# Additions out of PSUM in a seven-product down projection, marked urgent for VectorE's order

## The chip, the cores and the metric

The kernel runs on one core of one Trainium2 chip. The metric is the device time of one execution in microseconds (us), taken as the median of several runs. The core's engines each work through a queue of their own: TensorE (PE, with its weight loads as PEld), VectorE (DVE), ScalarE (ACT), GpSimd (POOL), and SyncE (SP), which issues the transfers. A scheduler in the programming layer fixes each queue's order when the program is built; at run time semaphores alone make one engine wait for another.

## What is computed

A two-layer encoder trunk over 512 + 256 tokens (two request groups, T = 768 columns here) of width 1024. Layer 0 mixes with a Fourier transform, layer 1 with a gated DeltaNet; after each mixer comes a SwiGLU channel mixer, whose second product the change touches:

```python
def swiglu(h, w_gu, w_down):
    gu = h @ w_gu
    return (jax.nn.silu(gu[..., :FFN_DIM]) * gu[..., FFN_DIM:]) @ w_down
...
        x = x + g2 * swiglu(h, ffn_w_gu[layer], ffn_w_down[layer])
```

FFN_DIM is 2816, 22 blocks of 128. `g2` is a gate per output column and request group.

## The kernel before

The residual x lies transposed in eight tiles of 128 x 768 (`xs`, called `x` in layer 0; in layer 1 the same eight are borrowed tiles, `pad`, `qT`, `vT`, `we`, `wa`). Every matrix product is made in three passes of reduced-precision parts: a weight block is split into `wh` (rounded by ScalarE) and `wl` (the rest, a subtraction on DVE); so is the activation.

The hidden blocks are worked in groups of four (`PARTS`). `gate_up` makes the gate and up blocks of one hidden block, "a unit": seven products instead of eight of a 2 x 2 block scheme, each 12 matmuls of 384 columns. `down4` then takes a group of four hidden blocks into four of the eight output blocks, again with seven products of a 2 x 2 scheme, named 1 to 7 and run in the order 1, 2, 6, 7, 5, 4, 3. Each product has two halves (`i`, two output blocks of 128) of 6 matmuls. A group needs two calls, `m0` = 0 and 4; the first runs after the first unit of the next group, the second after that group's second unit (`pending`). With five groups of four in layer 0 and four in layer 1 there are 18 calls.

The products add up in six PSUM banks: two each of `pw` (product 2), `py` (7, then 4 on top) and `px` (1, then 6, 5 and 3 on top). A product that goes on top may start in a bank only when the sum so far has been read out of it. `into` is the reader in question, on DVE: it multiplies the bank by the gate and adds it to x. `low(row)` is one addition of 384 columns (tokens 0 to 383), `high(row)` one of 128 and one of 256 (the two request groups in tokens 384 to 767). `shared` reads on ScalarE and adds on GpSimd.

DVE's queue holds, around a call: the weight splits of `down4` itself (line 498) and of the next unit (`split_w`, line 152), combinations of weight blocks (`comb`, lines 492 and 379, some of them on GpSimd), the activations' work of `gate_up` and `take`, and the additions of `into` (line 532 before, 533 after). Splits, combinations and ScalarE's reads are already built inside `tc.high_priority()`, which makes the scheduler take them first among those ready on an engine; the additions of `into` are not. Up to five weight blocks are held (`WP`), so a split may stand well ahead of its product.

Of the kernel before, what the change touches and what calls it, by code (L numbers as in the profile page):

```python
# [15 lines left out]
ALU = mybir.AluOpType  # L16
# [93 lines left out]
def encoder_kernel(  # L110
# [5 lines left out]
    V, A_, G = nc.vector, nc.scalar, nc.gpsimd  # L116
# [58 lines left out]
    def bank(pool, g=None):  # L175
        if pool.name == "ppr1":
            return pool.tile([P, SEGS[g][1]], F32, name=f"pr{g}", bufs=2 - g)
        return pool.tile([P, 512], F32, name="pr")

    def passes(ps, w, ah, al, first=True, **kw):  # L180

        kc = len(ah)
        for k in range(kc):
            for n, (a, b) in enumerate(((w[0], ah), (w[0], al), (w[1], ah))):
                last = mm(ps, a[k], b[k], start=(first and k == 0 and n == 0), stop=(k == kc - 1 and n == 2), **kw)
            yield last
# [18 lines left out]
    modT = const.tile([P, 14, KC, 2], F32, name="modT")  # L205
# [271 lines left out]
    def down4(l, c0, m0, rights, xs, psp, wk):  # L477

        w2d = ffn_w_down[l]

        def fetch2(m):
            stg = weights["stg"].tile([P, KC, P], F32, name="stg")
            nc.sync.dma_start(stg.rearrange("p (k m) n -> p k (m n)", m=2),
                              w2d[c0 * P : (c0 + 4) * P, m * P : (m + 2) * P].rearrange("(k p) n -> p k n", p=P))
            return stg.rearrange("p (k m) n -> p k m n", m=2)

        def four(t):
            return t.rearrange("p (k m) n -> p k m n", m=2)

        def comb(eng, out, a, b, op):  # L490
            with tc.high_priority():
                eng.tensor_tensor(out, a, b, op)

        def parts(src):
            wh, wl = (four(weights[name].tile([P, HK, P], F32R, name=name)) for name in ("wh", "wl"))
            with tc.high_priority():
                A_.copy(wh, src)  # L497
                V.tensor_tensor(wl, src, wh.bitcast(F32), ALU.subtract)  # L498
            return wh, wl

        def left():
            s_a, s_b = fetch2(m0), fetch2(m0 + 2)
            a11, a12, a21, a22 = s_a[:, 0::2], s_a[:, 1::2], s_b[:, 0::2], s_b[:, 1::2]
            yield parts(a11)
            yield parts(a12)
            s1 = four(wk.tile([P, HK, P], F32, name="s1", bufs=WS))
            comb(G, s1, a21, a22, ALU.add)
            comb(G, a21, a11, a21, ALU.subtract)
            comb(V, a11, s1, a11, ALU.subtract)
            yield parts(a11)  # L510
            yield parts(a21)
            yield parts(s1)
            yield parts(a22)
            comb(V, a12, a12, a11, ALU.subtract)
            yield parts(a12)

        lefts = left()
        pw, py, px = ([bank(psp) for _ in range(2)] for _ in range(3))
        gate = GATE[2 * l + 1]

        def run(n, ps, first, then):
            wh, wl = next(lefts)
            for i in range(2):
                for _ in passes(ps[i][:, :HT], ([wh[:, k, i] for k in range(2)], [wl[:, k, i] for k in range(2)]),
                                [r[n][0] for r in rights], [r[n][1] for r in rights], first, skip_group_check=True):
                    pass
                then(i, ps[i])

        def into(m, ps, a, b, g):
            x = xs[m][:, a:b]  # L530
            o = HT if a >= HT else 0
            V.scalar_tensor_tensor(x, ps[:, a - o : b - o], modT[:, gate, m, g : g + 1], x, ALU.mult, ALU.add)  # L532

        def low(row):
            return lambda i, ps: into(m0 + 2 * row + i, ps, 0, HT, 0)

        def high(row):
            def fn(i, ps):
                into(m0 + 2 * row + i, ps, HT, S0, 0)
                into(m0 + 2 * row + i, ps, S0, T, 1)  # L540
            return fn

        def shared(row):
            def fn(i, ps):
                m = m0 + 2 * row + i
                t = wk.tile([P, HT], F32, name="m7", bufs=M7)
                with tc.high_priority():
                    A_.activation(t, ps[:, :HT], AF.Copy, scale=modT[:, gate, m, 0:1])
                G.tensor_tensor(xs[m][:, LO], xs[m][:, LO], t, ALU.add)
            return fn  # L550

        run(1, px, True, shared(0))
        run(2, pw, True, low(0))
        run(6, px, False, shared(1))
        run(7, py, True, high(1))
        run(5, px, False, high(1))
        run(4, py, False, low(1))
        run(3, px, False, high(0))
# [65 lines left out]
    with ExitStack() as l0:  # L624
# [8 lines left out]
        with ExitStack() as fs:  # L633
# [41 lines left out]
            for c in range(KC):  # L675
                pcs.append(fp.tile([P, NC + NS], F32, name="xt", bufs=8))
                ps = pbig.tile([P, 1024], F32, name="big")
                oc, os_ = 0, 512
                for g, s in ((0, S0), (1, S1)):
                    for par in (0, 1):  # L680
# [3 lines left out]
                        for kt in range(nkt):  # L684
                            o, n = COLS[f"seq{g}_{kt}_{par}"]
# [13 lines left out]
            for c in range(KC):  # L699
# [7 lines left out]
                o, n = COLS["cosd"]  # L707
                mm(pf[:, 0:NC], ftab[:, o : o + n], y[:, :NC])
                o, n = COLS["sind"]
# [605 lines left out]
```

## Time and profile before

| | |
|---|---|
| median of 3 runs | 1961.96 us (1960.85 to 1962.16) |
| the profiled execution | 1961.55 us, span 1959.8 us |
| busy | PE 94%, PEld 84%, DVE 75%, ACT 50%, POOL 29% |
| mean granted TensorE clock | 0.984 |
| calls of `down4` in layer 0 | first at 257.9 us, last ends at 729.4 us |
| calls of `down4` in layer 1 | first at 1545.9 us, last ends at 1868.5 us |

A row of the timeline gives start and duration in us, engine, line, operation, output<-inputs by the program's names with buffer numbers left out, shapes, count, and in brackets the idle time before it and what ended that. `g` are the activations in `down4`'s matmuls, `pr` is any PSUM bank. Rows of "who waited" give us in total and times. A row of windows gives the stretch, its length, and for PE, PEld, DVE, ACT and POOL the busy time with the number of instructions, then the granted clock, the DMA engines' share and GB/s. Matmuls overlap: each is written some 0.34 us long, but the next starts 0.17 us after it.

### The profile page before, as it was taken

Reading aid. Unit: us, or ns where it says so; the run is one execution under the profiler, and the core shown is the slowest. Engines: PE = TensorE matmul, PEld = TensorE weight load, DVE = VectorE, ACT = ScalarE, POOL = GpSimd, SP = SyncE. Lnnn points to the kernel's source line nnn. Section 1 sums busy time; section 2 is a strip of 40 time slices with the busy share of each in tenths; the row PEclk is TensorE's granted clock in tenths of the full one; section 3 lists DMA queues with packets and bytes.
Section 4 is the critical chain, followed back from the end, with each engine's and each line's share of the span. In section 5 each row is a group of like instructions: output and inputs, shape, how many; then the busy total and the mean of one; then the engine's idle time right before and its main releaser. Section 6 shows DMA issues by size and latency. Waiting matters only on the chain.

```text
span 1959.8 us, 30027 instructions
## 1 busy us (share of the span) xinstructions
PE 1842.1 (94%) x11281; PEld 1636.7 (84%) x11281; DVE 1468.8 (75%) x2399; ACT 977.8 (50%) x1858; POOL 563.7 (29%) x454
## 2 busy tenths in 40 slices
PE   8899999999999998999999999899789999999998
PEld 5585998888897986888888888778589999999998
DVE  4638877777786767896887787773778888888875
ACT  3526544444443535756656557543554444444543
POOL 1314333233242310122213212320432333433431
PEclk9999999999999998999999999999899999999999
DMA  7654334433425434421222222241213222222211
GB/s 268 215 183 140 86 97 130 127 116 114 139 87 153 126 113 141 119 51 56 69 60 65 66 62 57 61 142 38 53 41 89 68 77 72 65 65 68 77 50 65
DMA packets 231914, 189.72 MB, mean 97 GB/s; under 512 B 20304, under 2 KB 200665, under 8 KB 231769
## 3 DMA queue, kind: packets, MB, share of 16 engines
q1 hardware_dynamic: 231360, 187.66, 31.7%
q8 instruction: 88, 1.44, 0.3%
q14 instruction: 57, 0.47, 0.1%
q10 hardware_dynamic: 409, 0.15, 0.0%
HBM read 174.36 MB, written 13.42 MB: 96 GB/s over the span
## 4 chain that ended last, share of the span: by engine, by line
PE 69%; DVE 14%; ACT 6%; DMA 5%; issue 3%; POOL 3%; ACTq 0%; SPq 0%; DVEq 0%; POOLq 0%
PE pr L132 58%; PE sm L132 8%; DVE wl L152 3%; DVE wa L913 2%; DMA at<-in_ada_w_dram 1%; PE ax L132 1%; DMA cc<-solved 1%; ACT wh L151 1%; POOL yy L1158 1%; DVE we L858 1%; PE big L132 1%; DVE x L532 1%; DVE tmp L1030 1%; ACT we L859 1%; DMA at<-in_final_ada_w_dram 1%
## 5 line engine op out<-in xcount | busy, mean ns | idle before, releaser
L132 PE MATMUL pr<-hh,wh 128*128 128x384 f32 (+2 forms) x1520 | 525.4, 348 | 9.0 <-ACT sg L403 2.3
L132 PE MATMUL pr<-hl,wh 128*128 128x384 f32 (+2 forms) x1520 | 522.8, 344 | 5.2 <-DVE hl L200 4.2
L132 PE MATMUL pr<-hh,wl 128*128 128x384 f32 (+2 forms) x1520 | 520.7, 343 | 1.2 <-DVE wl L152 1.2
L151 ACT CAST wh<-stg 128x512 fp32r<-128x512 f32 (+1 forms) x380 | 230.7, 609 | 394.7 <-PE pr L132 324.3
L152 DVE TENSOR_TENSOR wl<-stg,wh 128x512 fp32r<-128x512 f32 (+1 forms) x380 | 315.2, 832 | 127.7 <-ACT wh L151 124.7
L132 PEld LDWEIGHTS pr<-hh,wh 128*128 128x128 f32 x1520 | 287.7, 190 | 39.8 <-issue 7.4
L132 PEld LDWEIGHTS pr<-hl,wh 128*128 128x128 f32 x1520 | 288.2, 190 | 32.3 <-issue 9.5
L132 PEld LDWEIGHTS pr<-hh,wl 128*128 128x128 f32 x1520 | 287.9, 190 | 24.0 <-issue 6.2
L132 PE MATMUL pr<-g,wh 128*128 128x384 f32 (+2 forms) x1072 | 278.3, 341 | 23.6 <-DVE x L532 13.3
L132 PEld LDWEIGHTS pr<-g,wh 128*128 128x128 f32 x1072 | 191.8, 188 | 37.0 <-DVE x L532 19.8
L379 POOL TENSOR_TENSOR s<-stg 128x512 f32<-128x512 f32 x44 | 62.6, 1423 | 453.4 <-DMA stg<-in_ffn_w_gu_dram 362.7
L132 PE MATMUL pr<-el,wh 128*128 128x384 f32 x528 | 179.9, 341 | 6.4 <-POOL el L200 5.9
L132 PE MATMUL pr<-eh,wh 128*128 128x384 f32 x528 | 181.1, 344 | 3.7 <-ACT eh L199 3.7
L132 PE MATMUL pr<-g,wl 128*128 128x384 f32 (+2 forms) x536 | 181.1, 338 | 0.0
L132 PE MATMUL pr<-eh,wl 128*128 128x384 f32 x528 | 179.2, 339 | 0.0
L498 DVE TENSOR_TENSOR wl<-stg,wh 128x512 fp32r<-128x512 f32 x108 | 99.8, 924 | 36.0 <-ACT wh L497 33.8
L913 DVE SCALAR_TENSOR_TENSOR wa<-pad,cwT,wa 128x770 f32<-128x770 f32 x96 | 109.4, 1140 | 5.2 <-ACT wa L910 3.6
L132 PEld LDWEIGHTS pr<-eh,wh 128*128 128x128 f32 x528 | 100.2, 190 | 12.4 <-issue 7.0
L132 PEld LDWEIGHTS pr<-el,wh 128*128 128x128 f32 x528 | 99.9, 189 | 9.7 <-POOL el L200 8.5
L497 ACT CAST wh<-stg 128x512 fp32r<-128x512 f32 x108 | 67.1, 621 | 81.5 <-PE pr L132 67.1
L132 PEld LDWEIGHTS pr<-g,wl 128*128 128x128 f32 x536 | 101.0, 188 | 0.7
L132 PEld LDWEIGHTS pr<-eh,wl 128*128 128x128 f32 x528 | 99.8, 189 | 0.9 <-issue 0.8
(370 smaller groups left out, 3241.8 us busy)
## 6 DMA issues: line engine op xcount, KB each, us to landing
stg<-in_ffn_w_gu_dram SPq DMA_DIRECT2D x88, 512.0 KB, 4.7
at<-in_ada_w_dram SPq DMA_DIRECT2D x112, 256.0 KB, 3.1
at<-in_ada_w_dram SPq DMA_DIRECT2D x40, 512.0 KB, 4.6
stg<-in_ffn_w_down_dram SPq DMA_DIRECT2D x36, 512.0 KB, 3.7
stg<-in_gdn_w_in_dram SPq DMA_DIRECT2D x33, 512.0 KB, 4.3
at<-in_final_ada_w_dram SPq DMA_DIRECT2D x32, 256.0 KB, 3.6
raw<-gcd SPq DMA_DIRECT2D x8, 768.0 KB, 4.4
stg<-in_fnet_w_dram SPq DMA_DIRECT2D x8, 512.0 KB, 5.1
```

Of the source, the lines that this page charges most:

```text
L132: return nc.tensor.matmul(out, lhsT, rhs, start=start, stop=stop, **kw)
L151: A_.copy(wh[:, :n], src)
L152: V.tensor_tensor(wl[:, :n], src, wh[:, :n].bitcast(F32), ALU.subtract)
L379: eng.tensor_tensor(out, a, b, op)
L497: A_.copy(wh, src)
L498: V.tensor_tensor(wl, src, wh.bitcast(F32), ALU.subtract)
L532: V.scalar_tensor_tensor(x, ps[:, a - o : b - o], modT[:, gate, m, g : g + 1], x, ALU.mult, ALU.add)
L858: V.tensor_scalar(e, src, -44.0, None, ALU.max)
L859: A_.activation(e, e, AF.Exp, scale=-1.0)
L913: V.scalar_tensor_tensor(acc, pad[:, d : d + T + 2], wc[d], acc, ALU.mult, ALU.add)
L1030: se.tensor_tensor(t, r4[:, :, : k + 1, k : k + 1].to_broadcast(sh), u4[:, :, k : k + 1, k + 1 :].to_broadcast(sh), ALU.mult)
L1158: G.tensor_tensor(so, so, sq, ALU.add)
```

## The change

The addition in `into` is built inside `tc.high_priority()`.

```diff
         def into(m, ps, a, b, g):
             x = xs[m][:, a:b]
             o = HT if a >= HT else 0
-            V.scalar_tensor_tensor(x, ps[:, a - o : b - o], modT[:, gate, m, g : g + 1], x, ALU.mult, ALU.add)
+            with tc.high_priority():
+                V.scalar_tensor_tensor(x, ps[:, a - o : b - o], modT[:, gate, m, g : g + 1], x, ALU.mult, ALU.add)
```

Only DVE's queue stands otherwise than before; the rows of TensorE, ScalarE, GpSimd and SyncE follow each other as they did. DVE in the first call, from product 7's read-out to product 5's (`pr_2350` and `pr_2351` are `py`, `pr_2352` and `pr_2353` are `px`; `stg_2557`, `wl_2566` and `wl_2601` belong to the next unit); before:

```order
L532 SCALAR_TENSOR_TENSOR x_106<-pr_2350,modT_87,x_106 128x128
L379 TENSOR_TENSOR stg_2557<-s1_2596,stg_2557 128x512
L532 SCALAR_TENSOR_TENSOR x_106<-pr_2350,modT_87,x_106 128x256
L532 SCALAR_TENSOR_TENSOR x_106<-pr_2351,modT_87,x_106 128x128
L152 TENSOR_TENSOR wl_2566<-stg_2557,wh_2565 128x512
L532 SCALAR_TENSOR_TENSOR x_106<-pr_2351,modT_87,x_106 128x256
L379 TENSOR_TENSOR stg_2557<-stg_2557 128x512
L532 SCALAR_TENSOR_TENSOR x_106<-pr_2352,modT_87,x_106 128x128
L152 TENSOR_TENSOR wl_2601<-stg_2557,wh_2600 128x512
L532 SCALAR_TENSOR_TENSOR x_106<-pr_2352,modT_87,x_106 128x256
L532 SCALAR_TENSOR_TENSOR x_106<-pr_2353,modT_87,x_106 128x128
L532 SCALAR_TENSOR_TENSOR x_106<-pr_2353,modT_87,x_106 128x256
```

The same place now:

```order
L533 SCALAR_TENSOR_TENSOR x_106<-pr_2350,modT_87,x_106 128x128
L533 SCALAR_TENSOR_TENSOR x_106<-pr_2350,modT_87,x_106 128x256
L379 TENSOR_TENSOR stg_2557<-s1_2596,stg_2557 128x512
L533 SCALAR_TENSOR_TENSOR x_106<-pr_2351,modT_87,x_106 128x128
L533 SCALAR_TENSOR_TENSOR x_106<-pr_2351,modT_87,x_106 128x256
L533 SCALAR_TENSOR_TENSOR x_106<-pr_2352,modT_87,x_106 128x128
L533 SCALAR_TENSOR_TENSOR x_106<-pr_2352,modT_87,x_106 128x256
L152 TENSOR_TENSOR wl_2566<-stg_2557,wh_2565 128x512
L533 SCALAR_TENSOR_TENSOR x_106<-pr_2353,modT_87,x_106 128x128
L533 SCALAR_TENSOR_TENSOR x_106<-pr_2353,modT_87,x_106 128x256
L379 TENSOR_TENSOR stg_2557<-stg_2557 128x512
```

The two additions of a bank now stand together, and the split `wl_2566` and the second combination stand behind the read-out of the first `px` half instead of ahead of it.

DVE in the same call, from there to its last read-out (products 4 and 3); before:

```order
L532 SCALAR_TENSOR_TENSOR x_106<-pr_2350,modT_87,x_106 128x384
L152 TENSOR_TENSOR wl_2605<-stg_2559,wh_2604 128x512
L532 SCALAR_TENSOR_TENSOR x_106<-pr_2351,modT_87,x_106 128x384
L532 SCALAR_TENSOR_TENSOR x_106<-pr_2352,modT_87,x_106 128x128
L532 SCALAR_TENSOR_TENSOR x_106<-pr_2352,modT_87,x_106 128x256
L152 TENSOR_TENSOR wl_2635<-s1_2596,wh_2634 128x512
L532 SCALAR_TENSOR_TENSOR x_106<-pr_2353,modT_87,x_106 128x128
L532 SCALAR_TENSOR_TENSOR x_106<-pr_2353,modT_87,x_106 128x256
L152 TENSOR_TENSOR wl_2639<-stg_2559,wh_2638 128x512
```

The same place now:

```order
L533 SCALAR_TENSOR_TENSOR x_106<-pr_2350,modT_87,x_106 128x384
L533 SCALAR_TENSOR_TENSOR x_106<-pr_2351,modT_87,x_106 128x384
L152 TENSOR_TENSOR wl_2601<-stg_2557,wh_2600 128x512
L533 SCALAR_TENSOR_TENSOR x_106<-pr_2352,modT_87,x_106 128x128
L533 SCALAR_TENSOR_TENSOR x_106<-pr_2352,modT_87,x_106 128x256
L533 SCALAR_TENSOR_TENSOR x_106<-pr_2353,modT_87,x_106 128x128
L533 SCALAR_TENSOR_TENSOR x_106<-pr_2353,modT_87,x_106 128x256
L152 TENSOR_TENSOR wl_2605<-stg_2559,wh_2604 128x512
L152 TENSOR_TENSOR wl_2635<-s1_2596,wh_2634 128x512
L152 TENSOR_TENSOR wl_2639<-stg_2559,wh_2638 128x512
```

The splits of the next unit's third, fourth and fifth product (`wl_2601`, `wl_2605`, `wl_2635`) moved behind the additions of product 4, and the latter two behind those of product 3 as well. The other calls are rearranged in the same manner, the second of each group too.

## The prediction

> **What bounds the kernel now.** I read the page's busy times first, then who waits for the additions of line 532, then two of the eighteen calls of `down4` instruction by instruction.
>
> ```profile
> PE 1842.1 (94%) x11281; PEld 1636.7 (84%) x11281; DVE 1468.8 (75%) x2399; ACT 977.8 (50%) x1858; POOL 563.7 (29%) x454
> ...
>   PEld pr L132: 35.1, 38
>   PE pr L132: 23.5, 25
> ...
> 257.90:274.70 16.80, 15.01 (x89) 14.45 (x92) 14.92 (x24) 6.97 (x13) 9.07 (x7) 1.00 0.21 64
> 714.80:729.40 14.60, 14.60 (x88) 14.35 (x91) 11.82 (x23) 5.79 (x12) 5.16 (x4) 1.00 0.38 117
> ```
>
> TensorE is busy for 94% of the span, so the kernel gets shorter where a hole in its work closes. The two `pr` rows (who waited for line 532) are such holes: 25 waits of matmuls, 23.5 us, and 38 of their weight loads, 35.1 us. The windows are one call with such a wait and the one call without: the first is stretched to 16.80 us, though DVE works only 14.92 us in it (third pair of numbers). The granted clock is 1.00 in both, so the clock is no part of the difference.
>
> How much a call loses, from its first and last matmul (TensorE rows of the first call, of the sixth, and the only wait of the last):
>
> ```profile
> 257.89 0.51 PE L132 MATMUL pr<-g,wh 128*128 128x384 f32 x2
> 270.20 0.34 PE L132 MATMUL pr<-g,wl 128*128 128x384 f32 x1
> 272.32 0.62 PE L132 MATMUL pr<-g,wh 128*128 128x384 f32 x2 [1.79 <-DVE x L532]
> 274.34 0.34 PE L132 MATMUL pr<-g,wl 128*128 128x384 f32 x1
> ...
> 501.22 0.52 PE L132 MATMUL pr<-g,wh 128*128 128x384 f32 x2
> 515.50 0.62 PE L132 MATMUL pr<-g,wh 128*128 128x384 f32 x2 [0.62 <-DVE x L532]
> 517.75 0.34 PE L132 MATMUL pr<-g,wl 128*128 128x384 f32 x1
> ...
> 1867.17 0.62 PE L132 MATMUL pr<-g,wh 128*128 128x384 f32 x2 [0.30 <-DVE qT L532]
> ```
>
> A call has 84 matmuls, 12 for each of the seven products. Between 257.89 and 270.20 the first 72 start without a wait, 71 steps in 12.31 us: 0.1734 us a step. Undisturbed, first to last start would take 83 x 0.1734 = 14.39 us. The first call took 16.45 (2.06 lost, at one place), the sixth 16.53 (2.14 lost, in several smaller waits). A row's own "idle" understates it, because matmuls overlap: 1.79 is written where 270.20 to 272.32 is 2.12, or 1.95 more than a step, and the refill costs another 0.1. With 16 calls at 2.1, the last at 0.66 (0.30 idle, two refills) and one at nothing, the loss is about 34.3 us. That lies between the two totals above, near the weight loads' 35.1; those are the bounds I keep for the waits: 23.5 and 35.1.
>
> **Why TensorE waits there.** The product of `run(3, ...)` adds into the two `px` banks that `run(5, ...)` has just filled, so it may start only when DVE has read them. DVE in the first call:
>
> ```profile
> 265.50 0.34 DVE L532 SCALAR_TENSOR_TENSOR x<-pr,modT,x 128x128 f32<-128x128 f32 x1
> 265.76 1.24 DVE L379 TENSOR_TENSOR stg<-s,stg 128x512 f32<-128x512 f32 x1
> 266.93 0.73 DVE L532 SCALAR_TENSOR_TENSOR x<-pr,modT,x 128x256 f32<-128x256 f32 x2
> 267.58 0.68 DVE L152 TENSOR_TENSOR wl<-stg,wh 128x512 fp32r<-128x512 f32 x1
> 268.18 0.47 DVE L532 SCALAR_TENSOR_TENSOR x<-pr,modT,x 128x256 f32<-128x256 f32 x1
> 268.57 1.62 DVE L379 TENSOR_TENSOR stg<-stg 128x512 f32<-128x512 f32 x1
> 270.11 0.34 DVE L532 SCALAR_TENSOR_TENSOR x<-pr,modT,x 128x128 f32<-128x128 f32 x1
> 270.38 1.50 DVE L152 TENSOR_TENSOR wl<-stg,wh 128x512 fp32r<-128x512 f32 x1
> 271.80 1.65 DVE L532 SCALAR_TENSOR_TENSOR x<-pr,modT,x 128x256 f32<-128x256 f32 x4
> ```
>
> The first `px` half is complete when 54 of the matmuls have run: the last starts at 257.89 + 53 x 0.1734 = 267.08 and is done by 267.5. DVE reads its 128 columns at 270.11 and its 256 columns at 271.80 to 272.27; TensorE goes on at 272.32. Between 267.5 and 271.80 DVE spent its time on two weight splits (`wl`) and a combination (1.62) for the next unit, beside product 7's last addition.
>
> **The change part by part.** It adds and removes no arithmetic and no transfer; it reorders one engine. The four other queues stand as they were, so no DMA is issued in another order. DVE's own work is the same number of instructions of the same sizes.
>
> Replay of the first call with the new order and the steps of these rows (a 128-column addition moves the queue by 0.27, one of 256 by 0.39, a split by 0.60). Additions of product 7 first half 265.50 to 266.23; the combination, kept at its 1.24, to 267.40; product 7 second half to 268.1; product 5 first half to 268.8 (before: 272.27). Product 3 is due at 257.89 + 72 x 0.1734 = 270.38: no wait. Then the split, 0.60, or up to 1.5 as at 270.38, and the second half's additions: 270.1 or 271.0, due at 271.42: no wait. The 2.06 us go whole. I take 2.0 for each of the nine calls of this form (the first half of each group): 18 us.
>
> The second call of each group has more DVE work ahead. The sixth call, DVE and GpSimd:
>
> ```profile
> 509.05 1.50 DVE L152 TENSOR_TENSOR wl<-stg,wh 128x512 fp32r<-128x512 f32 x1
> 510.47 0.34 DVE L532 SCALAR_TENSOR_TENSOR x<-pr,modT,x 128x128 f32<-128x128 f32 x1
> 510.74 0.68 DVE L379 TENSOR_TENSOR stg<-s,stg 128x512 f32<-128x512 f32 x1
> 511.33 0.73 DVE L532 SCALAR_TENSOR_TENSOR x<-pr,modT,x 128x256 f32<-128x256 f32 x2
> 511.99 1.13 DVE L152 TENSOR_TENSOR wl<-stg,wh 128x512 fp32r<-128x512 f32 x1
> 513.04 0.47 DVE L532 SCALAR_TENSOR_TENSOR x<-pr,modT,x 128x256 f32<-128x256 f32 x1
> ...
> 511.25 1.31 POOL L379 TENSOR_TENSOR s<-stg 128x512 f32<-128x512 f32 x1 [1.25 <-DMA stg<-in_ffn_w_gu_dram]
> 512.64 1.61 POOL L379 TENSOR_TENSOR stg<-stg 128x512 f32<-128x512 f32 x1
> ```
>
> New order: product 7 first half 510.47 to 511.2 (product 4 due 501.22 + 60 x 0.1734 = 511.62); combination to 511.8; second half to 512.5 (due 512.66, with 0.2 for the hand-over a touch late); product 5 first half to 513.1 (due 513.70); the split until GpSimd's first operation, begun 0.5 later, is over, to 513.7; second half to 514.4 (due 514.75). What is left is 0.1 to 0.2 at one place. Calls whose DVE starts later into the additions keep up to 0.5. I take 0.4 for each of eight, 3.2 us, and give no credit for the call that lost nothing.
>
> What pays for it: the splits now behind the additions. In the first call `wl_2601` stood at 270.38 and is now behind both additions of product 4, `wl_2605` behind those of product 3. Product 4 would end at 270.5 and product 3 at 272.6. From 270.1, a combination of 1.62, product 4's two additions of 384 columns (0.60 each: the four of the 1.65 above less 0.39, 0.27 and 0.39) and a split of 0.60 make `wl_2601` ready at 273.5; product 3's four additions (1.32) and two more splits bring the next two at 275.4 and 276.0. Starting from 271.0 and with the first split at 1.5, these are 275.3, 277.2 and 277.8. The next unit needs them for its third, fourth and fifth product:
>
> ```profile
> 275.60 0.45 PE L132 MATMUL pr<-eh,wh 128*128 128x384 f32 x1
> 278.52 0.69 DVE L152 TENSOR_TENSOR wl<-stg,wh 128x512 fp32r<-128x512 f32 x1 [1.93 <-ACT wh L151]
> ```
>
> That unit began at 275.60, so now at about 273.6; a product is 12 x 0.1734 = 2.08, so they are wanted at 277.8, 279.8 and 281.9: 4.3 us to spare, 2.5 at worst, and DVE has 1.93 idle at 278.52. From below the cost is 0 (an earlier addition delays nothing that TensorE waits for now); from above, a wait as long as the first call's present one in each call, 2 us x 18, which is the slow rival. I take 0, since the spare exceeds every slow form of the rows.
>
> Sum: 34.3 - 3.2 = 31.1 us. The profiled execution took 1961.55 us (span 1959.8), 0.4 under the median of 1961.96; from the median, 1930.9, say 1931.
>
> One rule bears against this. The 1.13 us split at 511.99 ends 0.56 after GpSimd's first operation (511.25 + 1.31 = 512.56), and GpSimd's second, at 512.64, takes 1.61 where the first took 1.31: they take turns. The Trainium skill, SBUF — State Buffer, "SBUF: two separate sides", says that VectorE with two SBUF inputs and GpSimd lock one port pair for a whole instruction and that the loser waits for all of it. The rows agree; but the rule does not say who goes next when both wait, and if GpSimd goes twice the first rival below comes about, at its time instead of mine.
>
> **The rivals.**
> *The split that stands between the two halves of product 5 is held by GpSimd twice.* In the sixth call it would end 0.6 after 512.64 + 1.61 = 514.25, its additions at 515.6 instead of 514.75: 0.85 lost. Eight calls, 6.8 us: 1938. For it: splits of 1.50. Against it: the turn taken at 512.56.
> *The holes move on.* TensorE arrives earlier, and in layer 0 its conditioning products or the next unit's weights are not there yet. If the ten calls of layer 0 (9 x 2.1 = 19 us) give back 15 of it, 1946. For it: they share one queue. Against it: the queue's own waits in that layer are mostly for TensorE to be done with an older `at` tile (us, times, longest), so these transfers would come earlier too:
>
> ```profile
> SPq L253 <- PE sm L132: 206.3, 58, 13.0
> ```
>
> *DVE is the bound, whatever its order.* 14.92 us of DVE work against 14.56 of matmuls: if DVE could not catch up in the next unit, the call would keep its length, 1962. Against it: the 1.93 idle, and 75% over the span.
> *Slower: the weight splits come late.* DVE runs in order, so an urgent addition that waits for TensorE holds the splits behind it, and TensorE then waits for them. It decides once the splits are over 2.5 to 4.3 us later than worked out; to end 4 us above before, each call would need (31.1 + 4) / 18 = 1.95 us of new wait. At 3 us: 1931 + 54 = 1985.
>
> **How the numbers follow.** Forecast 0.64, held twice 0.16, moved on 0.10, DVE bound 0.06, late splits 0.04. The first three are faster (0.90); a measurement of this kernel tells about 0.2%, 4 us, from no change, so the fourth is "same". The low end is the whole 35.1 gone, 1927, less 1 for the spread of the runs; the high end takes in the moved holes with 1 us. 1926 to 1947 leaves the last two and the forecast's tails out.
>
> **What would show it.** In the new profile, waits of TensorE for line 533 under 5 us in all (25 waits, 23.5 before); a call's 84 matmuls in 14.4 to 15.0 us; DVE's busy time within 1%; no new row of TensorE waiting for `wl` in the gate and up products. It is wrong if such a row has more than 10 us, or if the call still takes 16 us with DVE never idle in it.

## The result and the profile after

| | before | after |
|---|---|---|
| median | 1961.95 us (1960.85 to 1962.16) | 1932.18 us (1929.79 to 1933.69) |
| profiled execution, span | 1961.55, 1959.8 us | 1933.2, 1931.5 us |
| layer 0, first matmul of the first call to the last of the last | 471.1 us | 452.3 us |
| the same in layer 1 | 322.3 us | 311.6 us |

The change makes the kernel faster by 1.5%: ratio 0.9848, 95% interval 0.9831 to 0.9865, or 29.8 us (26.5 to 33.2). 1931.0 was forecast. Of the 28.3 us between the two profiled executions, 18.9 lie in layer 0's calls and the units between them and 10.7 in layer 1's; the rest of the kernel is 1.2 us longer. All times and ratios here are of executions at a granted clock of 0.98 to 0.99; one, of the kernel before with added work, ran at 0.60 and took 2783 us, and is left out.

The page's busy times, and the rows of who waited for line 533:

```profile
PE 1831.6 (95%) x11281; PEld 1638.3 (85%) x11281; DVE 1452.7 (75%) x2399; ACT 977.6 (51%) x1858; POOL 563.6 (29%) x454
```

```profile
  POOL s L492: 6.2, 4
  ACT wh L151: 5.8, 4
  POOL s L379: 3.9, 2
  PEld pr L132: 0.2, 1
```

The two rows of TensorE's waits, 23.5 us for matmuls and 35.1 for weight loads, have shrunk to 0.2 us. The other three, waits of GpSimd and ScalarE, have grown (6.9 us before), but inside the calls TensorE waits for neither engine. The windows of the first and the last call of layer 0, as shown of before:

```profile
258.30:273.00 14.70, 14.70 (x89) 14.45 (x92) 12.75 (x22) 6.94 (x13) 9.08 (x7) 1.00 0.23 73
696.35:710.95 14.60, 14.60 (x88) 14.35 (x91) 11.79 (x23) 5.78 (x12) 5.13 (x4) 1.00 0.38 117
```

The window that was 16.80 us long is now 14.70, about as long as that of the call that had no wait. Its first and last matmuls, and the one that first uses the split `wl_2601`:

```profile
258.30 0.51 PE L132 MATMUL pr<-g,wh 128*128 128x384 f32 x2
272.68 0.34 PE L132 MATMUL pr<-g,wl 128*128 128x384 f32 x1
...
280.12 0.33 PE L132 MATMUL pr<-hh,wl 128*128 128x384 f32 x1
```

From 258.30 to 272.68 are 14.38 us, 83 steps of 0.1733: no hole is left. DVE in this call:

```profile
265.90 0.73 DVE L533 SCALAR_TENSOR_TENSOR x<-pr,modT,x 128x128 f32<-128x128 f32 x2
266.56 0.85 DVE L379 TENSOR_TENSOR stg<-s,stg 128x512 f32<-128x512 f32 x1
267.33 1.38 DVE L533 SCALAR_TENSOR_TENSOR x<-pr,modT,x 128x128 f32<-128x128 f32 x4
268.63 1.62 DVE L152 TENSOR_TENSOR wl<-stg,wh 128x512 fp32r<-128x512 f32 x1
270.18 0.73 DVE L533 SCALAR_TENSOR_TENSOR x<-pr,modT,x 128x128 f32<-128x128 f32 x2
270.83 1.13 DVE L379 TENSOR_TENSOR stg<-stg 128x512 f32<-128x512 f32 x1
271.88 1.13 DVE L533 SCALAR_TENSOR_TENSOR x<-pr,modT,x 128x384 f32<-128x384 f32 x2
272.93 0.68 DVE L152 TENSOR_TENSOR wl<-stg,wh 128x512 fp32r<-128x512 f32 x1
```

The four additions at 267.33 are product 7's second half and product 5's first half. They end at 268.7 and product 3 is due at 258.30 + 72 x 0.1734 = 270.8: 2.1 us to spare, where before the last of them was 1.9 us too late (272.27 for 270.38). The split at 268.63 (`wl_2566`), which stood ahead of the last addition of product 7, now stands behind them all.

### The profile page after: what moved, and what is told of

Read it like the earlier page. It is cut to its first block, busy times and chain, and to the rows that moved or that the text cites. A ratio compares the mean times of both kernels' runs of the same rounds, so it can differ in the third digit from the quotient of the medians.

```text
span 1931.5 us, 30045 instructions
## 1 busy us (share of the span) xinstructions
PE 1831.6 (95%) x11281; PEld 1638.3 (85%) x11281; DVE 1452.7 (75%) x2399; ACT 977.6 (51%) x1858; POOL 563.6 (29%) x454
## 4 chain that ended last, share of the span: by engine, by line
PE 68%; DVE 14%; ACT 7%; DMA 5%; issue 4%; POOL 3%; SPq 0%; DVEq 0%; ACTq 0%; POOLq 0%
PE pr L132 57%; PE sm L132 8%; DVE wa L914 2%; DVE wl L152 2%; DMA at<-in_ada_w_dram 2%; PE ax L132 1%; ACT wh L151 1%; DMA cc<-solved 1%; POOL yy L1159 1%; DVE we L859 1%; PE big L132 1%; ACT g L352 1%; ACT we L860 1%; DVE tmp L1031 1%; DVE x L533 1%
## 5 line engine op out<-in xcount | busy, mean ns | idle before, releaser
L152 DVE TENSOR_TENSOR wl<-stg,wh 128x512 fp32r<-128x512 f32 (+1 forms) x380 | 308.3, 814 | 114.2 <-ACT wh L151 112.2
L132 PE MATMUL pr<-g,wh 128*128 128x384 f32 (+2 forms) x1072 | 273.7, 337 | 0.0
```

The lines of the kernel that those rows point to most:

```text
L132: return nc.tensor.matmul(out, lhsT, rhs, start=start, stop=stop, **kw)
L152: V.tensor_tensor(wl[:, :n], src, wh[:, :n].bitcast(F32), ALU.subtract)
```

## Experiments

Each run was compared with the kernel before on the same chip. The *order* theory says that only what stands ahead of a read-out in DVE's queue counts; in its rivals DVE's load, or one product's read-out alone, decides.

**One part of the change alone: product 5's additions.**

```diff
+                urgent[0] = n == 5
...
+            with tc.high_priority() if urgent[0] else nullcontext():
```

> Only the additions of product 5 (the run into the px banks that product 3 adds onto) are urgent; those of products 1, 2, 6, 7, 4 and 3 are not. Order theory (what counts is what stands ahead of the read-out that the next product in the same bank needs): the splits and combinations that product 5's additions now pass have to stand somewhere, and in the first call they land ahead of the 256-column addition of product 7's second half, which product 4 needs. The hole closes at product 3 and opens at product 4: by the durations of the first call (two splits and a combination, some 3.3 us of DVE ahead of it) it is as large as before or larger, so 1970 to 1990 us, slower than before by 0.4 to 1.4%. Rival (only product 5's read-out was ever late, the other additions need no priority): the whole gain, about 1932 us.

Measured: 1960.58 us (1959.08 to 1966.2), ratio 0.9996 [0.9985, 1.0007]: no change. The gain of this part alone is nothing, as the order theory has it, but the loss it forecast did not come. In time the two forms of the hole came out the same. DVE in the fifth call and the only wait of TensorE there:

```profile
472.89 0.73 DVE L536 SCALAR_TENSOR_TENSOR x<-pr,modT,x 128x128 f32<-128x128 f32 x2
473.54 1.22 DVE L379 TENSOR_TENSOR stg<-stg 128x512 f32<-128x512 f32 x1
474.69 0.34 DVE L536 SCALAR_TENSOR_TENSOR x<-pr,modT,x 128x128 f32<-128x128 f32 x1
474.95 1.50 DVE L152 TENSOR_TENSOR wl<-stg,wh 128x512 fp32r<-128x512 f32 x1
476.37 2.56 DVE L536 SCALAR_TENSOR_TENSOR x<-pr,modT,x 128x256 f32<-128x256 f32 x6
```

```profile
476.90 0.62 PE L132 MATMUL pr<-g,wh 128*128 128x384 f32 x2 [1.10 <-DVE x L536]
```

The two at 472.89 are product 5's first half, done 11.0 us after the call's first matmul instead of 14.2. The combination and the split they passed now hold back the 256 columns of product 7's second half (the first of the six at 476.37), and product 4's second half waits for those. The scheduler also moved TensorE's rows here: product 3's first half runs ahead of product 4's second, and up to eight matmuls of other work stand in a call. So the size of the new hole is not that of the order of DVE alone. All waits of TensorE for line 536 sum to 23.3 us (27), as before the change (23.5).

**All but product 5.** The same edit with `n != 5`.

> All of the additions are urgent except those of product 5. Order theory: the hole at product 3 stays, since the splits and the combination still stand ahead of product 5's read-out; worked out as 2 to 3 us in each of 17 calls, so 1960 to 1972 us: no gain. Rival (the gain comes from the additions as a whole, for instance because DVE and GpSimd hold each other up less): most of the gain stays, 1935 to 1945 us.

Measured: 1964.7 us (1962.36 to 1967.65), ratio 1.0018 [1.0004, 1.0031]: no gain. TensorE waits 27.4 us (19 times) for line 536. DVE in the fifth call:

```profile
473.19 0.34 DVE L536 SCALAR_TENSOR_TENSOR x<-pr,modT,x 128x128 f32<-128x128 f32 x1
473.46 1.68 DVE L379 TENSOR_TENSOR stg<-stg 128x512 f32<-128x512 f32 x1
475.06 1.76 DVE L152 TENSOR_TENSOR wl<-stg,wh 128x512 fp32r<-128x512 f32 x1
476.74 1.52 DVE L536 SCALAR_TENSOR_TENSOR x<-pr,modT,x 128x384 f32<-128x384 f32 x3
```

```profile
477.79 0.62 PE L132 MATMUL pr<-g,wh 128*128 128x384 f32 x2 [1.69 <-DVE x L536]
```

The two halves of one read-out (128 columns at 473.19, 256 in the group at 476.74) are torn apart by 3.4 us of a combination and a split, and by an urgent addition of product 4. Here too TensorE's rows moved, more than above: up to 23 matmuls of other work stand in a call. So the size is again not that of DVE's order alone, but the rival, that making most additions urgent brings most of the gain, has fallen: neither part brings anything, both together 1.5%.

**More work at the same place, before and after.** Two additions of weight 0 behind product 5's first half in every call:

```diff
+                if twice and i == 0:
+                    zero(m0 + 2 * row + i, ps, HT, S0)
+                    zero(m0 + 2 * row + i, ps, S0, T)
...
+        run(5, px, False, high(1, True))
```

> The kernel before, with two more additions behind product 5's first half in each call (weight 0, 128 and 256 columns, so that x stays as it is): 0.66 us more of DVE in each of 18 calls, 12 us in all. Order theory: they stand in the chain that product 3 waits for, which has no slack, so each call takes 0.6 to 1.0 us longer: 1973 to 1980 us. Rival (DVE's load as such decides, not the place): the same cost here as in the changed kernel.

> The changed kernel with the same two additions of weight 0 (urgent as well) behind product 5's first half. Order theory: product 3 now has about 1.6 us to spare at this place in the first call of a group and 0.4 to 0.6 in the second, so the cost is near nothing in nine calls and 0.1 to 0.4 in the others: 1932 to 1938 us. Rival (DVE's load decides): the same 11 to 18 us as in the kernel before, 1943 to 1950 us.

Measured: on the kernel before 1968.41 us, ratio 1.0042 [1.0027, 1.0057], slower by 8.2 us (5.3 to 11.2), with 28.1 us of matmul waits for line 532 (25) where there were 23.5; on the changed kernel 1928.03 us, ratio 0.9832 [0.9815, 0.9849], against 0.9848 without the additions. The same 0.5 to 0.6 us of DVE a call costs the first kernel time and the second none, so it is the place in the chain and not DVE's load. The first cost came out under the 11 to 18 expected, and here too the scheduler had moved TensorE's rows and filled part of the hole with up to 15 other matmuls a call, so this run gives the sign of the cost and not its size. That the second became no slower but, if anything, 3 us faster was not expected by either theory; the next part explains it.

**Each layer alone**, and the changed kernel once more on that chip (`urgent[0] = l == 0` or `l == 1`):

> The changed kernel again, on the chip of the runs that follow, so that they are compared with it there. Both theories: 1930 to 1934 us.

> The additions are urgent in layer 0 alone. Theory (each call's loss is its own): the ten calls of layer 0 give what the profiles show there, 18.9 us, and layer 1 stays as it was: 1943 us (1941 to 1945). Rival (the two layers share a limit, so that a part is given back later): less than 15 us, 1947 us or more.

> The additions are urgent in layer 1 alone: the eight calls of layer 1 give what the profiles show there, 10.7 us: 1951 us (1949 to 1953). With the run of layer 0 alone the two gains should add up to that of the whole change, 29.8 us. Rival (what layer 1 gave back, some 3 us, comes from layer 0's being earlier): up to 14 us here, 1948 us.

Measured: both layers 1930.04 us, 0.9848 [0.9833, 0.9862]; layer 0 alone 1945.46, 0.9918 [0.9903, 0.9933]; layer 1 alone 1946.61, 0.9934 [0.9919, 0.9949]. The gains, 0.82% and 0.66%, add up to 1.48% against 1.52%, so no shared limit shows. In these three kernels TensorE's, ScalarE's and GpSimd's rows follow each other as before, all 11281 matmuls included, so the order of DVE's queue alone makes the gain. The single gains, 16.1 us (13.1 to 19.0) and 12.9 (10.0 to 15.9), are less and more than the 18.9 and 10.7 expected, and the second is nearer its rival's 14; the stretches of the profile, which leave out the scatter of the rest of the kernel, side with the theory. In the profiled runs layer 0's stretch was 452.1 us (before 471.1) and layer 1's 311.2 (before 322.3). First to last matmul, the calls of layer 0 take 20.1 us less than before and those of layer 1 14.0. Layer 0's stretch gains nearly all of it (18.9 and 19.0), layer 1's only 10.7 and 11.1: 3 us are missing there, in both kernels in which layer 1 is changed.

**Where those 3 us went.** In the changed kernel one row of TensorE's waits is new, and it is the only one between the first and the last call of layer 1:

```profile
PE pr L132 <- ACT up L403: 1.6, 3, 0.8
```

The first of the three, on TensorE, ScalarE and DVE:

```profile
1581.05 0.45 PE L132 MATMUL pr<-hh,wh 128*128 128x384 f32 x1 [0.38 <-ACT up L403]
...
1579.26 0.83 ACT L199 CAST g<-sg 128x768 fp32r<-128x768 f32 x1 [0.54 <-DVE sg L471]
1580.00 0.61 ACT L151 CAST wh<-stg 128x512 fp32r<-128x512 f32 x1
1580.52 0.47 ACT L403 COPY up<-pr 128x384 f32<-128x384 f32 x1
...
1576.54 0.68 DVE L152 TENSOR_TENSOR wl<-stg,wh 128x512 fp32r<-128x512 f32 x1
1577.14 0.55 DVE L470 TENSOR_TENSOR sg<-sg 128x384 f32<-128x384 f32 x1
1577.61 0.55 DVE L434 TENSOR_TENSOR sg<-pr,sg 128x384 f32<-128x384 f32 x1
1578.08 0.68 DVE L152 TENSOR_TENSOR wl<-stg,wh 128x512 fp32r<-128x512 f32 x1
1578.68 0.55 DVE L471 TENSOR_TENSOR sg<-sg 128x384 f32<-128x384 f32 x1
```

The bank that TensorE wants is read by ScalarE's copy to `up` at 1580.52. That stands in ScalarE's queue behind a cast that waits for DVE's line 471, and line 471 stands behind the splits that the additions have passed. Before, the same copy began 7.5 us after the last matmul of the call (1601.66, the call's last at 1594.13); now it begins 8.6 us after it (1571.90). The test exchanges two conversions, so that the cast which does not wait for line 471 comes first and the copy stands ahead of the other:

```diff
-        split_to(*t42, sb)
         split_to(*t13, sa)
+        split_to(*t42, sb)
```

> The changed kernel with the last two conversions of right() exchanged, so that ScalarE's cast that does not wait for line 471 stands first. Theory of the new wait (in layer 1 of the changed kernel TensorE waits three times for ScalarE's read-out of up, 1.6 us, because that stands behind a cast that waits for DVE): the read-out now stands ahead of that cast, the three waits go and with them 2 to 3 us, so 1929 to 1930.5 us against the changed kernel's 1932. Rival (what layer 1 gave back is the slower pace of the matmuls alone, or noise): the same time as the changed kernel within 1 us.

> The changed kernel with the two conversions exchanged once more, since five rounds left the time of the whole kernel open (the stage of layer 1 was 2.7 us shorter). Theory of the new wait: ratio to before 0.983 to 0.984, 2 to 3 us under the changed kernel's 0.9848. Rival: 0.985.

ScalarE at the same place:

```profile
1578.37 0.47 ACT L403 COPY up<-pr 128x384 f32<-128x384 f32 x1
1579.08 0.84 ACT L199 CAST g<-sg 128x768 fp32r<-128x768 f32 x1 [0.24 <-DVE sg L471]
```

The copy now stands ahead of the waiting cast. In both profiled runs TensorE has no wait of layer 1's calls left, and layer 1's stretch is 308.5 us in both, 2.7 to 3.1 us less than in the two of the changed kernel (311.6 and 311.2). That makes 13.8 us less than before, nearly all of the 14.0 by which its calls had become shorter. Of the 3.1 us between 311.6 and 308.5, 2.5 are the three gaps, from start to start of the matmuls, and 0.6 a slower pace of the matmuls, so the rival (the pace alone) fails here. The theory of the new wait holds in its place. In the time of the whole kernel it shows less clearly: 1929.72 us, 0.9843 [0.9827, 0.9859], which is within 1 us of the changed kernel's 1930.04 on that chip, as the rival had it, and the second time 1928.06, 0.983 [0.9816, 0.9845].

The kernel with the zero additions had no such wait either and 308.4 us in layer 1, which accounts for its being faster than the changed kernel. That agrees with the cause: there the scheduler had itself put the copy ahead of that cast, at the places of all three waits and nowhere else in ScalarE's queue in layer 1's calls and units, while TensorE's rows there stood as before:

```profile
1577.46 0.47 ACT L403 COPY up<-pr 128x384 f32<-128x384 f32 x1
1577.92 1.57 ACT L199 CAST g<-sg 128x768 fp32r<-128x768 f32 x2
```

**How late may the splits be?** Passes `x*0 + x` behind each call's last addition, eight of them:

```diff
+            for _ in range(8 if i else 0):
+                x = xs[m0 + 1][:, HT:]
+                with tc.high_priority():
+                    V.scalar_tensor_tensor(x, x, 0.0, x, ALU.mult, ALU.add)
```

> The changed kernel with four passes over one tile of x on DVE behind each call's last addition (x*0 + x, 384 columns, urgent, x stays as it is), each about 0.47 us as line 470 is: the weight splits of the next unit come 1.9 us later. Theory (the splits behind the additions have 4.3 us to spare, 2.5 at worst): TensorE does not wait for them, 0 to 0.3 us a call, 1932 to 1937 us. Rival (the splits are ready only just in time, and their moving behind the additions costs already): about 1.9 us in each of 17 calls, 1962 us or more.

> The same with eight passes, 3.8 us: more than the 2.5 us to spare at worst and a little less than the 4.3. Theory: waits of TensorE for wl appear in the calls that have the least to spare, 0.5 to 1.5 us in each of about nine, 1936 to 1948 us. Rival (the splits are ready only just in time): 3.8 us in each of 17 calls, 1995 us. A second rival (the spare is much larger than worked out): as with four passes, 1932 to 1935 us.

Measured: four passes 1928.41 us, 0.983 [0.9808, 0.9852]; eight 1933.82 us, 0.9862 [0.9845, 0.9878]. DVE was busy 67.9 us longer with eight (1520.6 us), and the time hardly changed. The waits in layer 1 with eight:

```profile
PE pr L132 <- ACT up L403: 4.1, 3, 1.6
PE pr L132 <- DVE qT L533: 0.2, 1, 0.2
```

No wait for `wl` appeared in the calls and units of either, so the second rival is nearest, but the runs do not measure the spare: the scheduler put the splits between the passes, so that the first three behind the second call of layer 1 had none, one and two of eight passes ahead of them. With four the time came out even under the forecast, since the wait for `up` was gone (ScalarE's copy again stood ahead of the cast) and layer 1's stretch 309.4. With eight a wait for `up` of 4.1 us stands at another place, in the second unit behind a group's second call (the first at 1592.27), and layer 1's stretch is 315.1 instead of 311.6.

**A faster version.** The exchange, and lines 434 and 448, the two other additions out of PSUM, urgent too:

> The exchanged conversions, and the other additions out of PSUM on DVE, lines 434 and 448 in gate_up, urgent as well. Theory: the sums that a product waits for now all pass the splits; TensorE waits only a few us for them in the changed kernel, so the gain is small: 0 to 2 us under the exchanged conversions alone, 1927 to 1930 us. Rival (what must come first once more pushes splits behind): 1 to 3 us over it.

Measured: 1924.76 us (1921.72 to 1929.62), ratio 0.9815 [0.9795, 0.9835]; 1920.0 us was the profiled span. It is the fastest of all, 2 us better than expected, though its interval still touches that of the change alone. What it gains over the exchange alone is not placed: layer 0's stretch was 449.6 us (452.4 and 452.6 with the exchange alone) and layer 1's 309.3 (308.5), TensorE's rows stood in another order in places, and the stretch from the last call of layer 0 to the first of layer 1, which holds seven units with line 434, took 813.5 us here and 813.2 to 818.6 in the other profiled runs.

## Why the prediction was right

- **The loss and its cause** held. All 18 calls of before, measured from first to last matmul against 83 steps of 0.1735, lost 36.2 us where 34.3 was worked out; the 2.1 us a call was read from two calls, and the third and fourth lost 3.5 and 3.0. After the change 2.2 us are left. That it is the order of DVE's queue is shown by the layer runs, in which no other engine's rows moved; that it takes both products together, by the sign of the two part runs.
- **The residual of 3.2 us in the second calls** was not there. Those calls take 14.4 to 14.7 us without a hole. The replay's times were right (product 5's first half done 0.6 us before product 3 is due, in the sixth call and in its replay); the lateness that it added, 0.2 us for a hand-over and then 0.4 a call, shows in none of them. The sixth, DVE and GpSimd, and the split of the fourteenth:

```profile
498.46 0.73 DVE L533 SCALAR_TENSOR_TENSOR x<-pr,modT,x 128x128 f32<-128x128 f32 x2
499.11 0.68 DVE L379 TENSOR_TENSOR stg<-s,stg 128x512 f32<-128x512 f32 x1
499.71 1.38 DVE L533 SCALAR_TENSOR_TENSOR x<-pr,modT,x 128x128 f32<-128x128 f32 x4
501.02 0.67 DVE L152 TENSOR_TENSOR wl<-stg,wh 128x512 fp32r<-128x512 f32 x1
...
499.35 1.59 POOL L379 TENSOR_TENSOR s<-stg 128x512 f32<-128x512 f32 x1 [1.36 <-DMA stg<-in_ffn_w_gu_dram]
501.02 1.83 POOL L379 TENSOR_TENSOR stg<-stg 128x512 f32<-128x512 f32 x1
...
1657.97 1.14 DVE L152 TENSOR_TENSOR wl<-stg,wh 128x512 fp32r<-128x512 f32 x1
...
1657.25 1.32 POOL L379 TENSOR_TENSOR s<-stg 128x512 f32<-128x512 f32 x1 [2.30 <-DMA stg<-in_ffn_w_gu_dram]
1658.65 1.62 POOL L379 TENSOR_TENSOR stg<-stg 128x512 f32<-128x512 f32 x1
```

- **GpSimd holds the split twice**: not so here. In the sixth call GpSimd's first operation ends at 500.94, and the split, which comes up at 501.02, takes 0.67. In the fourteenth it comes up during that operation, ends 0.54 us after it (1659.11 against 1658.57) and goes ahead of GpSimd's second, so it is lengthened once, to 1.14 us. Where it took longest, 1.73 us in the last call, it too ended 0.55 us after GpSimd's first. This time is written as busy and not as a wait, so semaphores are not all that holds up an engine here. The four additions at 499.71 ran at their usual pace beside GpSimd. That agrees with the Trainium skill, SBUF — State Buffer, "SBUF: two separate sides", by which a VectorE instruction contends with GpSimd only in a two-port mode or with two SBUF inputs (of the two tiles that these add, one lies in PSUM).
- **Late splits at no cost** held for what TensorE waits for: `wl_2601` was ready at 272.93 + 0.68 = 273.6 (273.5 worked out) and used at 280.12, 6.5 us later instead of 4.3. TensorE's waits for `wl` are the same 1.2 us (2) in both profiles.
- **The step that failed** is the same one, read further: it put the cost of the moved splits at 0, having asked only who waits for them, and not what else in DVE's queue stands behind them. Line 471 does, ScalarE's cast waits for it, and the read-out of `up` waits behind the cast. That was worth 2.7 to 3.1 us. In the profiles the calls became 34.0 us shorter, and 5.7 of it came back: 3.3 in layer 1, 1.2 in layer 0 and 1.2 in the rest of the kernel, which scatters by more than that from run to run. A loss worked out too small and a residual that was not there made up for half of it, so it is partly luck that 31.1 us forecast and 29.8 measured agree better than their terms.
- **The holes move on in layer 0**: only 1.2 us of 20.1 were given back, for instance in these waits, of which before had 0.5 us:

```profile
PE sm L264 <- DVE av L260: 1.3, 2, 1.1
PE sm L132 <- DMA at<-in_ada_w_dram: 0.9, 3, 0.3
PE sm L132 <- DMA at<-in_final_ada_w_dram: 0.5, 1, 0.5
```

- **DVE is the bound** fell: 12.75 us of work in the first call's window instead of 14.92, and eight passes more in every call, 67.9 us of DVE, cost 2.7 us by the ratios, which their intervals do not tell from nothing. DVE's total went down by 16.1 us, 1.1% and not "within 1%": line 379's combinations, for one, took 7.4 us less (82.1 for 89.5 in 88). That fewer of them met an operation of GpSimd is likely, but was not counted.

## What to carry to other kernels

When an accumulating bank is read by an engine that also prepares weights, give the read-outs the higher priority as a whole: one product's alone only moved the hole to the next bank. A queue's order is costed by everything behind the moved instructions and by who waits for that on a third engine. A part run whose order the scheduler changes on TensorE as well tells the sign and not the size.

## Not expected of the hardware

Matmuls of 384 columns run at more than one pace at a granted clock of 1.00. One call in layer 1, beside the 14.38 us of the first:

```profile
1706.41 0.52 PE L132 MATMUL pr<-g,wh 128*128 128x384 f32 x2
1721.07 0.34 PE L132 MATMUL pr<-g,wl 128*128 128x384 f32 x1
```

14.66 us over 83 steps are 0.1766 us a step instead of 0.1733, with no hole. In the changed kernel one stretch of this pace began at the wait at 1670.27 and ended at that of 1759.95, but it comes and goes elsewhere too, in layer 0 as well (the fourth call took 14.67 us). Five calls took 14.50 us, 0.1747 a step, so there are not just two paces. What sets them was not tried.
